# Splitting the second layer's weights: channel factors multiplied in place, 512 columns at once

## The chip, the cores and the metric

The kernel runs on one core of a Trainium2 chip. A core has a matrix engine (TensorE, PE in the profile; PEld is its loading of weights), a vector engine (VectorE, DVE), an activation engine (ScalarE, ACT), a general engine (GpSimd, POOL) and a queue engine that issues most of the transfers (SyncE, SP). Each engine works through its own list of instructions in order and waits on semaphores. The metric is the device time of one execution in microseconds, the median of several runs.

## The reference, cut to what matters

The reference is one step of a two-layer encoder over 1024 prompt tokens and 32 sample tokens (1056 in all), with 1024 channels. Layer 0 mixes tokens by pooling, layer 1 by differential attention; both attend to 256 memory tokens and end in a squared-ReLU MLP. Everything is float32.

```
h = rmsnorm(x, g_attn[l]);  z = h @ w_in[l]            # every layer
kv = rmsnorm(x, g_kv) @ w_kv                           # before layer 1: shared keys and values
rmsnorm(x, g) = x * rsqrt(mean(x*x) + 1e-6) * g        # g: one factor for each of the 1024 channels
```

In layer 1 the same x is normalised with two different sets of factors, `g_kv` for `w_kv` and `g_attn[1]` for `w_in[1]`. A factor on an input channel may as well be put on the row of the weight that this channel meets, and the factor of a token (the rsqrt) on the product. The kernel does so in layer 1: x is split once without factors, and each weight is multiplied by its column of factors.

## The kernel before, in words

TensorE multiplies float32 numbers in three passes. Each operand is split into a high part (`hi`, the number rounded to the type that TensorE reads, F32R) and a low part (`lo = number - hi`), and `mm3` (L48 to L54) issues hi·hi, hi·lo and lo·hi. The tokens lie in three groups of 352 columns (GW); a weight tile gives 128 output rows, from two halves of 128 x 512 numbers, which hold four blocks of 128 input channels each.

A weight goes through three stages. `weight_load` (L94) takes the next weight from the list in `weights` (L60) and starts the transfer of its two halves into buffers called `wraw`, of which there are six. `weight_split` (L121) calls `part` (L103) on each half: it writes `whi` and `wlo`, of which there are eight each. `weight` (L129) hands the split weight to the matmuls. A `wraw` buffer is free for the next transfer when the last instruction that reads it, the one that writes `wlo`, is done.

For most weights `part` is two instructions on 512 columns: a copy on ScalarE (L111) and a subtraction on VectorE (L112). For the 16 weights of layer 1 that carry factors (8 of `w_kv`, 8 of `w_in`, L78 to L84) it goes through the four blocks of a half one by one: ScalarE multiplies 128 columns by the factor and rounds (L116), VectorE multiplies again and subtracts (L117). The factor is one number for each partition and block, from the table `gains`.

The order of the instructions on each engine is set by a scheduler from the program's order, its data and its own estimates of durations; TensorE's order is fixed by it too. When an edit changes instructions, the scheduler may interleave all engines anew. The stages that matter here, in microseconds from the start of the profiled span:

- to about 930: the MLP of layer 0. Its last row of weights is split by L112, `b` at L1336 adds two partial sums of hidden activations.
- 930 to 975: the last part of the second MLP product (`ff2_last`): L1492 adds each finished tile to x, L57 and L58 split x into `xh` and `xl` for layer 1, L202 and L203 sum squares for the norm. The first `w_kv` halves are already loaded here. L1505 stores x to DRAM on the same SP queue that loads the weights.
- 975 to 1190: layer 1's projections and the differential attention. `diff_project` makes keys (`kst`, L722), values (`vst`, L734) and queries (`qf`, L743) from the PSUM tiles `dn`; these projections are the fill between score matmuls (L827, L828), transposes (L869) and products with values. VectorE makes the softmax's inputs (L834, L808) and the low parts `aTl` of the transposed probabilities (L58); ScalarE does the exponentials (L836) and the high parts `aTh` (L57). L212 makes the sums for the norms.

Of the kernel before, what the change touches and what calls it, by code (L numbers as in the profile page):

```python
# [10 lines left out]
F32 = mybir.dt.float32  # L11
F32R = mybir.dt.float32r
AF = mybir.ActivationFunctionType
ALU = mybir.AluOpType
# [29 lines left out]
class Kern:  # L44
# [58 lines left out]
    def part(self, src, eng, gcol=None):  # L103

        if self.wplace:
            hi, lo = self.wplace.pop(0), self.wplace.pop(0)
        else:
            hi = self.wpool.tile([128, 4, 128], F32R, tag="whi", name="whi", bufs=NW)
            lo = self.wpool.tile([128, 4, 128], F32R, tag="wlo", name="wlo", bufs=NW)
        if gcol is None:  # L110
            self.nc.scalar.copy(hi, src)  # L111
            eng.tensor_tensor(lo, src, hi.bitcast(F32), ALU.subtract)  # L112
            return hi, lo
        for c in range(4):
            gain = self.gains[:, gcol + c:gcol + c + 1]
            self.nc.scalar.mul(hi[:, c], src[:, c], gain)  # L116
            eng.scalar_tensor_tensor(lo[:, c], src[:, c], gain, hi[:, c].bitcast(F32), ALU.mult, ALU.subtract)  # L117
        return hi, lo

    def weight_split(self):  # L120
# [84 lines left out]
    def rstd(self, acc, n, r=None, pool=None, tile=None):  # L205

        nc = self.nc
        acc = acc if isinstance(acc, list) else [acc]
        N = acc[0].shape[-1]
        ps = (tile or self.stile)()[:, :N]  # L210
        for i, part in enumerate(acc):
            nc.tensor.matmul(ps, lhsT=self.ones, rhs=part, start=i == 0, stop=i == len(acc) - 1)  # L212
        y = (pool or self.base).tile([128, N], F32, tag="rs_y", name="rs_y", bufs=1)
        nc.scalar.activation(y, ps, AF.Ln, bias=self.epsc, scale=1.0 / n)
        nc.scalar.activation(y, y, AF.Exp, scale=-0.5)
        nc.vector.scalar_tensor_tensor(ps, ps, n * EPS, y, ALU.add, ALU.mult)
        nc.vector.scalar_tensor_tensor(ps, ps, -0.5 / n, y, ALU.mult, ALU.mult)
        nc.vector.scalar_tensor_tensor(ps if r is None else r, ps, 1.5, y, ALU.add, ALU.mult)
        return ps
# [1040 lines left out]
    def plan_weights(self, kind, b, at, loads, sums, parts):  # L1260


        nc = self.nc
        S = {}

        def raw(k):
            return self.raws[kind, b, k]

        def add(k):
            S[k] = S[2] if k == 4 else self.ph.tile([128, 4, 128], F32, tag="ws", name="ws", bufs=3)  # L1270
            x, y, op = ((2, 3, ALU.add), (1, 0, ALU.subtract), (0, 2, ALU.subtract), (1, 2, ALU.subtract))[k - 1]
            x = S[1] if k == 2 else raw(x)
            y = S[2] if k == 4 else raw(y)
            nc.vector.tensor_tensor(S[k], x, y, op)

        def part(k):
            src = S[int(k[1])] if k[0] == "S" else raw(("A11", "A12", "A21", "A22").index(k))
            self.A[kind, b, k] = self.part(src, self.low(kind, k))

        for k, o in enumerate(loads):  # L1280
            self.job(at + o, lambda k=k: self.block(kind, b, k))
        for k, o in enumerate(sums):
            self.job(at + o, lambda k=k: add(k + 1))
        for k, o in parts:
            self.job(at + o, lambda k=k: part(k))
# [424 lines left out]
```

## Time and profile before

| | us |
|---|---|
| median of 3 runs (2095.39 to 2095.83) | 2095.4 |
| the profiled execution, its own time | 2095.72 |
| span from its first to its last instruction | 2093.9 |
| TensorE busy | 2072.7 (99%) |
| VectorE busy | 1681.0 (80%) |
| ScalarE busy | 1125.8 (54%) |
| GpSimd busy | 567.3 (27%) |

The span is 1.8 us shorter than the execution's own time. Busy is the time in which an engine ran an instruction; one duration can overlap the next on the same engine, so the distance from start to start of neighbours is often shorter than the duration. Idle time of an engine costs nothing unless the engine that sets the end waits for it. Lines named L with a number are lines of the kernel before; the changed kernel has three lines fewer, so what stands below the change is there numbered three lower.

### The profile page before, as it was taken

Reading aid. Unit: us, or ns where it says so; the run is one execution under the profiler, and the core shown is the slowest. Engines: PE = TensorE matmul, PEld = TensorE weight load, DVE = VectorE, ACT = ScalarE, POOL = GpSimd, SP = SyncE. Lnnn points to the kernel's source line nnn. Section 1 sums busy time; section 2 is a strip of 40 time slices with the busy share of each in tenths; the row PEclk is TensorE's granted clock in tenths of the full one; section 3 lists DMA queues with packets and bytes.
Section 4 is the critical chain, followed back from the end, with each engine's and each line's share of the span. In section 5 each row is a group of like instructions: output and inputs, shape, how many; then the busy total and the mean of one; then the engine's idle time right before and its main releaser. Section 6 shows DMA issues by size and latency. Waiting matters only on the chain.

```text
span 2093.9 us, 35115 instructions
## 1 busy us (share of the span) xinstructions
PE 2072.7 (99%) x12961; PEld 2032.1 (97%) x12961; DVE 1681.0 (80%) x3156; ACT 1125.8 (54%) x2437; POOL 567.3 (27%) x577
## 2 busy tenths in 40 slices
PE   9999999999999999999999999999999999999997
PEld 8998999999999999999999998999999999999997
DVE  8856598888888888868778877588888888888865
ACT  7546364444444444456777766355444454444454
POOL 1021113343333333220111212104334333433323
PEclk9999999999999999999999999999999999999999
DMA  5635321111111111124222212411111111111112
GB/s 192 204 114 159 126 61 59 44 56 46 51 51 48 55 46 56 42 71 162 75 80 80 83 46 91 161 51 53 60 41 58 44 56 46 51 51 51 51 41 83
DMA packets 88140, 156.83 MB, mean 75 GB/s; under 512 B 12704, under 2 KB 29728, under 8 KB 87456
## 3 DMA queue, kind: packets, MB, share of 16 engines
q1 hardware_dynamic: 85952, 149.47, 22.3%
q10 hardware_dynamic: 2016, 5.13, 0.8%
q8 instruction: 101, 1.65, 0.3%
q14 instruction: 71, 0.58, 0.1%
HBM read 126.64 MB, written 23.72 MB: 72 GB/s over the span
## 4 chain that ended last, share of the span: by engine, by line
PE 89%; DVE 3%; ACT 3%; DMA 1%; issue 1%; POOL 0%; SPq 0%; DVEq 0%; ACTq 0%; POOLq 0%
PE dn L54 15%; PE dn L52 15%; PE dn L53 15%; PE mm L52 9%; PE mm L53 9%; PE mm L54 9%; PE xb L52 3%; PE xb L54 3%; PE xb L53 3%; PE sc L52 1%; PE sc L827 1%; PE sc L54 1%; PE sc L53 1%; PE mm L869 1%; PE sc L828 1%
## 5 line engine op out<-in xcount | busy, mean ns | idle before, releaser
L52 PE MATMUL dn<-xh,whi 128*128 128x352 f32 x1168 | 383.3, 328 | 3.0 <-ACT mvs L348 1.3
L54 PE MATMUL dn<-xh,wlo 128*128 128x352 f32 x1168 | 378.6, 324 | 0.0
L53 PE MATMUL dn<-xl,whi 128*128 128x352 f32 x1168 | 378.3, 324 | 0.2 <-DVE xl L233 0.2
L112 DVE TENSOR_TENSOR wlo<-wraw,whi 128x512 fp32r<-128x512 f32 x344 | 278.6, 813 | 86.9 <-ACT whi L111 86.1
L111 ACT CAST whi<-wraw 128x512 fp32r<-128x512 f32 x344 | 212.7, 620 | 233.4 <-PE dn L53 111.6
L1403 DVE TENSOR_TENSOR x<-x,mm 128x352 f32<-128x352 f32 x560 | 287.5, 513 | 63.1 <-PE mm L54 63.1
L52 PE MATMUL mm<-h2h,whi 128*128 128x352 f32 x832 | 270.4, 325 | 0.0
L54 PE MATMUL mm<-h2h,wlo 128*128 128x352 f32 x832 | 268.0, 322 | 0.0
L53 PE MATMUL mm<-h2l,whi 128*128 128x352 f32 x832 | 266.4, 320 | 0.0
L111 ACT CAST whi<-ws 128x512 fp32r<-128x512 f32 x232 | 143.8, 620 | 221.0 <-PE dn L53 123.4
L1403 DVE TENSOR_TENSOR x<-x,xb 128x352 f32<-128x352 f32 x448 | 222.9, 512 | 26.1 <-PE xb L54 23.4
L52 PEld LDWEIGHTS dn<-xh,whi 128*128 128x128 f32 x1168 | 219.5, 188 | 8.6 <-issue 2.1
L53 PEld LDWEIGHTS dn<-xl,whi 128*128 128x128 f32 x1168 | 220.7, 189 | 2.8 <-DVE xl L233 0.9
L54 PEld LDWEIGHTS dn<-xh,wlo 128*128 128x128 f32 x1168 | 220.1, 188 | 0.4
L58 POOL TENSOR_TENSOR h2l<-t,h2h 128x352 fp32r<-128x352 f32 x112 | 136.2, 1217 | 171.6 <-ACT h2h L57 171.6
L112 DVE TENSOR_TENSOR wlo<-ws,whi 128x512 fp32r<-128x512 f32 x232 | 179.2, 772 | 3.5 <-ACT whi L111 3.5
L58 POOL TENSOR_TENSOR h2l<-b,h2h 128x352 fp32r<-128x352 f32 x92 | 116.2, 1277 | 228.8 <-PE mm L54 204.1
L1387 POOL TENSOR_TENSOR t<-b,b 128x352 f32<-128x352 f32 x56 | 64.6, 1154 | 366.3 <-ACT b L1306 366.3
L53 PEld LDWEIGHTS mm<-h2l,whi 128*128 128x128 f32 x832 | 156.3, 188 | 0.4
L52 PEld LDWEIGHTS mm<-h2h,whi 128*128 128x128 f32 x832 | 156.1, 188 | 0.4
L54 PEld LDWEIGHTS mm<-h2h,wlo 128*128 128x128 f32 x832 | 156.2, 188 | 0.0
L54 PE MATMUL dn<-T,wlo 128*128 128x352 f32 x480 | 155.7, 324 | 0.0
(322 smaller groups left out, 5275.9 us busy)
## 6 DMA issues: line engine op xcount, KB each, us to landing
wraw<-in_w_ff SPq DMA_DIRECT2D x256, 256.0 KB, 2.6
wraw<-in_w_out SPq DMA_DIRECT2D x44, 256.0 KB, 3.6
wraw<-in_w_in SPq DMA_DIRECT2D x30, 256.0 KB, 3.5
o<-oscr SPq DMA_DIRECT2D x36, 176.0 KB, 3.2
xscr<-x SPq DMA_DIRECT2D x3, 1408.0 KB, 5.4
wraw<-in_w_mem SPq DMA_DIRECT2D x16, 256.0 KB, 3.0
wraw<-in_w_memv SPq DMA_DIRECT2D x16, 256.0 KB, 3.0
wraw<-in_w_kv SPq DMA_DIRECT2D x16, 256.0 KB, 2.9
```

Of the source, the lines that this page charges most:

```text
L52: mm(ps, lhsT=ah, rhs=bh, start=first, stop=False, skip_group_check=more)
L53: mm(ps, lhsT=ah, rhs=bl, start=False, stop=False, skip_group_check=more)
L54: self.last_mm = mm(ps, lhsT=al, rhs=bh, start=False, stop=last, skip_group_check=more)
L58: (lo_eng or self.nc.vector).tensor_tensor(lo, src, hi.bitcast(F32), ALU.subtract)
L111: self.nc.scalar.copy(hi, src)
L112: eng.tensor_tensor(lo, src, hi.bitcast(F32), ALU.subtract)
L827: nc.tensor.matmul(o, lhsT=q[:, c, 0, qc], rhs=KS[:, c, k:k + n], start=True, stop=False)
L828: nc.tensor.matmul(o, lhsT=q[:, c, 1, qc], rhs=KS[:, c, k:k + n], start=False, stop=True)
L869: nc.tensor.transpose(pt[:, 256 * a + 128 * i:256 * a + 128 * i + 128], A[i][:, k:k + 128], self.ident)
L1387: self.nc.gpsimd.tensor_tensor(h[out], h[a], h[c], ALU.subtract)
L1403: nc.vector.tensor_tensor(xj, xj, ps, ALU.add)
```

## The change

For a weight with factors, `part` now first multiplies the whole half (512 columns) by its factors on VectorE, in place in `wraw`; the factors are read with each one repeated over 128 columns. Then it copies to `whi` on ScalarE and subtracts into `wlo` on VectorE, as for every other weight.

```diff
         else:
             hi = self.wpool.tile([128, 4, 128], F32R, tag="whi", name="whi", bufs=NW)
             lo = self.wpool.tile([128, 4, 128], F32R, tag="wlo", name="wlo", bufs=NW)
-        if gcol is None:
-            self.nc.scalar.copy(hi, src)
-            eng.tensor_tensor(lo, src, hi.bitcast(F32), ALU.subtract)
-            return hi, lo
-        for c in range(4):
-            gain = self.gains[:, gcol + c:gcol + c + 1]
-            self.nc.scalar.mul(hi[:, c], src[:, c], gain)
-            eng.scalar_tensor_tensor(lo[:, c], src[:, c], gain, hi[:, c].bitcast(F32), ALU.mult, ALU.subtract)
+        if gcol is not None:
+            gain = self.gains[:, gcol:gcol + 4].unsqueeze(2).broadcast_to([128, 4, 128])
+            eng.tensor_tensor(src, src, gain, ALU.mult)
+        self.nc.scalar.copy(hi, src)
+        eng.tensor_tensor(lo, src, hi.bitcast(F32), ALU.subtract)
         return hi, lo
```

In the changed kernel the multiplication is line 112, the copy line 113 and the subtraction line 114. The scheduler interleaves anew. On VectorE, at the end of layer 0's MLP, where the last rows of its weights are split (`wlo<-wraw,whi`) and the last hidden sums `b` are added, there stands before:

```order
L1403 TENSOR_TENSOR x_2680<-x_2680,xb 128x352 x2
L112 TENSOR_TENSOR wlo<-wraw,whi 128x512 x2
L1336 TENSOR_TENSOR b_10646<-u_10624,dn 128x352
L112 TENSOR_TENSOR wlo<-wraw,whi 128x512
L1336 TENSOR_TENSOR b_10701<-u_10535,dn 128x352
L112 TENSOR_TENSOR wlo<-wraw,whi 128x512 x3
L1492 TENSOR_TENSOR x_2682<-x_2682,mm 128x352
```

and in the changed kernel, with the same names and lines three lower:

```order
L114 TENSOR_TENSOR wlo<-wraw,whi 128x512
L112 TENSOR_TENSOR wraw<-wraw,gains 128x512 x3
L1333 TENSOR_TENSOR b_10701<-u_10535,dn 128x352
L114 TENSOR_TENSOR wlo<-wraw,whi 128x512 x2
L112 TENSOR_TENSOR wraw<-wraw,gains 128x512
L114 TENSOR_TENSOR wlo<-wraw,whi 128x512
L112 TENSOR_TENSOR wraw<-wraw,gains 128x512
L1489 TENSOR_TENSOR x_2682<-x_2682,mm 128x352
L1489 TENSOR_TENSOR x_2682<-x_2682,dn 128x352
L58 TENSOR_TENSOR xl_10753<-x_2682,xh_10752 128x352
L112 TENSOR_TENSOR wraw<-wraw,gains 128x512
```

Six multiplications of layer 1's first three weights have moved up here; three of them stand ahead of the last sum `b`, two between the last splits and one after the first addition to x. All wait for the transfers of their halves. On VectorE again, where layer 1 begins and the first keys `kst` are taken from PSUM, there stands before:

```order
L203 TENSOR_TENSOR acc_10750<-acc_10750,sq 128x352
L58 TENSOR_TENSOR xl_11096<-x_2681,xh_11095 128x352
L117 SCALAR_TENSOR_TENSOR wlo<-wraw,gains,whi 128x128 x22
L275 TENSOR_SCALAR gsub<-gains 128x1
L722 TENSOR_TENSOR kst<-dn,rs_11003 128x352
L722 TENSOR_TENSOR kst<-dn,rs_11165 128x352
L779 TENSOR_TENSOR KS<-kst,KS 64x256
```

and in the changed kernel:

```order
L58 TENSOR_TENSOR xl_11086<-x_2681,xh_11085 128x352
L114 TENSOR_TENSOR wlo<-wraw,whi 128x512 x2
L112 TENSOR_TENSOR wraw<-wraw,gains 128x512 x3
L114 TENSOR_TENSOR wlo<-wraw,whi 128x512
L112 TENSOR_TENSOR wraw<-wraw,gains 128x512 x2
L272 TENSOR_SCALAR gsub<-gains 128x1
L719 TENSOR_TENSOR kst<-dn,rs_10993 128x352
L719 TENSOR_TENSOR kst<-dn,rs_11155 128x352
L112 TENSOR_TENSOR wraw<-wraw,gains 128x512 x2
```

Ahead of the first `kst` stand eight instructions of 512 columns in place of 22 of 128 columns, and two more multiplications stand behind the second `kst`. Further on, to about 1190 us, the multiplications stand one or two at a time between the softmax's instructions, and TensorE's order differs in where single projection matmuls stand between score and value matmuls; no matmul is added or removed.

## Rows read from the trace of the kernel before

**Rows 1.** The page, part 1: busy us of each engine, share, instructions.
```profile
PE 2072.7 (99%) x12961; PEld 2032.1 (97%) x12961; DVE 1681.0 (80%) x3156; ACT 1125.8 (54%) x2437; POOL 567.3 (27%) x577
```

**Rows 2.** Busy time by stretches: stretch, length, then each engine's busy us.
```profile
core 0: us, PE busy (x) PEld busy (x) DVE busy (x) ACT busy (x) POOL busy (x), PEclk, DMA share, GB/s
960.00:1190.00 230.00, 227.59 (x1461) 220.01 (x1460) 184.17 (x490) 167.93 (x439) 33.81 (x65) 1.00 0.33 101
```

**Rows 3.** Waits of PE, 960 to 1190: us in total, times, longest.
```profile
PE mm L53 <- DVE aTl L58: 0.7, 2, 0.4
PE mm L800 <- DVE std L841: 0.6, 1, 0.6
PE dn L52 <- DVE kst L722: 0.5, 1, 0.5
PE sc L827 <- DVE std L834: 0.2, 1, 0.2
PE mm L52 <- ACT aTh L57: 0.2, 1, 0.2
```

**Rows 4.** Lines L116 and L117: shortest, median, longest ns; first, last start.
```profile
L116 ACT ACTIVATE whi<-wraw,gains x128: 383/390/408, 964.6 to 1185.7; 128x128 fp32r<-128x128 f32 x128
L117 DVE SCALAR_TENSOR_TENSOR wlo<-wraw,gains,whi x128: 329/344/892, 965.1 to 1186.2; 128x128 fp32r<-128x128 f32 x128
```

**Rows 5.** Timeline of DVE and ACT: start, us, engine, line, how many merged.
```profile
976.17 3.34 ACT L116 ACTIVATE whi<-wraw,gains 128x128 fp32r<-128x128 f32 x11
...
976.81 5.86 DVE L117 SCALAR_TENSOR_TENSOR wlo<-wraw,gains,whi 128x128 fp32r<-128x128 f32 x22
...
1014.75 0.69 DVE L58 TENSOR_TENSOR V<-mm,V 128x512 fp32r<-128x512 f32 x1
1015.35 0.47 DVE L808 SCALAR_TENSOR_TENSOR pr<-pr,std 128x256 f32<-128x256 f32 x1
```

**Rows 6.** Lines L111, L112 and L912: shortest, median, longest ns.
```profile
L111 ACT CAST whi<-wraw x344: 602/620/661, 3.9 to 2033.3; 128x512 fp32r<-128x512 f32 x172
L112 DVE TENSOR_TENSOR wlo<-wraw,whi x344: 673/692/1439, 4.6 to 2034.0; 128x512 fp32r<-128x512 f32 x172
...
L912 DVE TENSOR_TENSOR sb<-sc,dists x1: 757/757/757, 1236.4 to 1236.4; 128x576 f32<-128x576 f32 x1
```

**Rows 7.** Waits of all engines, 960 to 1190: ScalarE's copies for a buffer.
```profile
ACT whi L116 <- PE dn L53: 7.8, 8, 4.0
```

**Rows 8.** Transfers issued from 915 to 930: KB each, median us to landing.
```profile
wraw<-in_w_kv SPq DMA_DIRECT2D x4, 256.0 KB, 2.9
```

**Rows 9.** Timeline of DVE, 916 to 931, end of layer 0's MLP.
```profile
919.08 0.69 DVE L112 TENSOR_TENSOR wlo<-wraw,whi 128x512 fp32r<-128x512 f32 x1
922.45 0.52 DVE L1336 TENSOR_TENSOR b<-u,dn 128x352 f32<-128x352 f32 x1 [2.69 <-PE dn L54]
...
929.78 0.52 DVE L1492 TENSOR_TENSOR x<-x,mm 128x352 f32<-128x352 f32 x1 [2.37 <-PE mm L54]
```

**Rows 10.** Timeline of ACT over the same stretch.
```profile
923.01 0.50 ACT L1305 ACTIVATE b<-b 128x352 f32<-128x352 f32 x1 [0.16 <-DVE b L1336]
...
926.06 0.62 ACT L111 CAST whi<-wraw 128x512 fp32r<-128x512 f32 x1 [0.98 <-PE dn L53]
```

**Rows 11.** Timeline of DVE and PE where layer 1's first keys are taken.
```profile
982.65 0.94 DVE L722 TENSOR_TENSOR kst<-dn,rs 128x352 f32<-128x352 f32 x2
...
983.22 0.43 PE L52 MATMUL dn<-xh,whi 128*128 128x352 f32 x1 [0.49 <-DVE kst L722]
```

**Rows 12.** Line L1274: ns; idle before it until a transfer (us, times).
```profile
L1274 DVE TENSOR_TENSOR ws<-wraw x116: 675/940/1436, 294.0 to 1995.4; 128x512 f32<-128x512 f32 x116
...
  DMA wraw<-in_w_ff: 22.6, 28
```

## The prediction

> **What bounds the kernel now.** I read the page's busy times first. TensorE is busy for 2072.7 of 2093.9 us, VectorE for 80% and ScalarE for 54% [rows 1]. So the end is set by TensorE's list of matmuls, and an edit that adds or removes no matmul can shorten the run only by time in which TensorE waits. Next I looked where the touched lines run: both start between 964.6 and 1186.2 us [rows 4]. In the stretch 960 to 1190 TensorE is busy for 227.59 of 230 us, VectorE for 184.17, ScalarE for 167.93, and the granted clock is 1.00 [rows 2]. TensorE is idle for 2.4 us there, and the table of its waits accounts for 2.2 of them: 0.7, 0.6, 0.5 and 0.2 us on VectorE's results, 0.2 us on ScalarE's [rows 3]. None of these waits is for `whi` or `wlo`. The split weights are always ready in time; what the change lightens, TensorE does not wait for.
>
> **The work taken away and put in.** 16 weights of two halves are 32 halves. Before, each takes four instructions on each of two engines: 128 on ScalarE and 128 on VectorE [rows 4]. After, ScalarE has 32 copies, and VectorE 32 multiplications and 32 subtractions.
>
> ScalarE: eleven L116 in a row take 3.34 us, 0.304 us from one to the next [rows 5], so 128 are 38.9 us. A copy of 512 columns takes 0.62 us [rows 6], 32 are 19.8 us. ScalarE saves some 19 us. TensorE can get from that at most the 0.2 us that it waited for ScalarE [rows 3]; ScalarE's work otherwise lies beside matmuls.
>
> VectorE: 22 L117 in a row take 5.86 us, 0.266 us each [rows 5]; 128 are 34.1 us. A subtraction on 512 columns lasts 0.692 us [rows 6], but the next instruction behind one of that size starts 0.60 us after it (1014.75 to 1015.35) [rows 5], so 64 take 38.4 us: 4.3 us more. Six of the multiplications now stand around 930 us, outside the stretch; in the stretch it is 58 x 0.60 = 34.8 us against 34.1, which is 0.7 us more on an engine that has 45.8 us idle there [rows 2]. The multiplication itself isn't in the trace of before. Its lower bound is the 0.692 us of a subtraction of the same size; as upper bound I take the longest of those, 1.439 us [rows 6]. The nearest row to a repeated operand is L912, which reads one operand twice over (once for each half of its columns): 576 columns in 0.757 us, against 0.692 us for 512 without repetition [rows 6], so 65 ns for 64 more columns and nothing for the repetition. I take 0.692 us (0.60 from start to start). At the upper bound 26 multiplications in the stretch cost VectorE 26 x 0.75 = 19.5 us more.
>
> Finer grain lost: what stands behind one of the new instructions waits up to 0.60 - 0.27 = 0.33 us longer than behind an L117. If that hit each of the five waits of TensorE [rows 3] it would cost 1.7 us; if the new order removes them all, it gains 2.2. I take +0.4 us.
>
> From the moment a `whi` buffer is free, a half took four L116 and the last L117, 4 x 0.304 + 0.344 = 1.6 us; now it takes a copy and a subtraction, 0.62 + 0.69 = 1.3 us, since the multiplication needs no `whi` and can be done earlier. ScalarE waited eight times, 7.8 us in all, for such a buffer [rows 7]. So weights come some 0.3 us sooner there, and `wraw` buffers come free as much sooner. As TensorE waits for neither, this is worth 0.
>
> **The multiplications that moved up.** This is where the change adds waits. The third one ahead of `b` needs a half whose buffer comes free when the subtraction that starts at 919.08 ends, at 919.77 [rows 9]. The transfer lands 2.9 us later [rows 8], at 922.7, and the multiplication ends about 0.6 us after that, 923.3. Behind it in VectorE's list stands `b`, which started at 922.45 [rows 9]: it comes 0.85 us late. ScalarE's L1305 waited for it at 923.01 and then had 0.98 us idle before 926.06, where it waits for TensorE [rows 10]. The delay is smaller than that idle time, so ScalarE meets TensorE at 926.06 as before, and what TensorE needs next comes as before. With the cover gone it would cost up to 0.85 us; I take 0. The multiplications between the last splits delay the last `wlo` by about a microsecond; its matmuls belong to the second half of the output tiles, and VectorE's next duty is at 929.78, for which it waited 2.37 us [rows 9]. I take 0.
>
> **The first keys of layer 1.** Before, 22 L117 stand ahead of `kst` at 982.65, and TensorE waits 0.49 us for it [rows 11]. Now there are eight instructions, 8 x 0.60 = 4.8 us in place of 5.86, so `kst` could come 1.1 us earlier and the 0.49 us would go. But the last two of the five multiplications wait for halves whose buffers come free only shortly before, and a transfer takes 2.9 us [rows 8]; that may put them a microsecond late. Between -0.5 and +1.0 I take 0.
>
> A rule that speaks against the change: the two-input instructions share something with GpSimd. The trace has L112 at 0.692 us in the median and 1.439 at the longest, L117 at 0.344 and 0.892 [rows 4, 6], and GpSimd is busy for 33.81 of the 230 us [rows 2]. The Trainium skill (SBUF — State Buffer, "Who interferes with whom") says that a VectorE instruction with two SBUF inputs and a GpSimd instruction that reads SBUF exclude each other for the whole instruction, so that longer ones block longer; by it, the estimate is 58 x 0.15 x 0.75 = 6.5 us lost on VectorE here. The same estimate for the 128 L117 is 128 x 0.15 x 0.55 = 10.6 us, so the rule's own difference favours the change, and TensorE would see little of either.
>
> **The sum.** Against the profiled execution's own 2095.72 us: ScalarE's relief -0.1 (0 to -0.2), VectorE's grain and load +0.4 (-2.2 to +2.4, which is 1.7 + 0.7), the moved multiplications 0 (0 to +0.85), the first keys 0 (-0.5 to +1.0). That is 2096.0. The profiled execution lies 0.3 us above the median of 2095.4, so in runs I expect 2095.7 to 2096; I say 2096.0. The bounds added up give 2092.8 to 2100.0 with all on one side; the likeliest case's own range is 2094 to 2099.
>
> **The rivals.**
> Same, as worked out: 80%. I call "same" what lies within 0.2%, 4.2 us, of 2095.4 (2091.2 to 2099.6); a measurement of this kernel can hardly tell less.
>
> Slower, multiplications that wait at the head of VectorE's list: a multiplication is now the first reader of a fresh half, so a late transfer stops VectorE, and with it PSUM tiles that TensorE needs emptied; before, ScalarE stood in front. What speaks for it: L1274, which reads fresh halves on VectorE too, waited 28 times in 116 for the transfer, 22.6 us in all, 0.81 us each time [rows 12]. Against: the scheduler has put the multiplications where the half should be there, and VectorE has idle time. The place is the attention stage after 1010 us, where by the order 14 multiplications stand among the softmax's instructions. If all of them waited 0.81 us and TensorE paid in full, it is 11.3 us, 2107; at half of them 5.7 us, 2101.5, which I take for this case. It decides from the point where one wait is longer than TensorE's lead over the PSUM tile behind it. 13%.
>
> Slower, the repeated factors are read slowly: 1.439 us in place of 0.692. That takes 19.5 of VectorE's 45.8 idle us; TensorE pays perhaps a quarter, as an estimate, and the time is 2101, at most 2115. Against it stands L912. 4%.
>
> Faster beyond 0.2%: all of TensorE's idle time in the stretch is 2.4 us, which gives 2093.3 and is still "same". More would need stages whose order barely changed to run better. 3%.
>
> **The numbers.** Faster 0.03, same 0.80, slower 0.13 + 0.04 = 0.17. The range has to hold the first case and reach into the slower ones: 2093.5 to 2103. Below it lies perhaps 0.05, above it about 0.09.
>
> **What the profile of the changed kernel would show.** Right: 32 copies of about 0.62 us and 64 two-operand instructions of about 0.69 us on VectorE; in 960 to 1190 ScalarE's busy time down by some 20 us, VectorE's within a few us of 184, TensorE's idle time still 1 to 5 us. `b` starts near 923.3 with a multiplication waiting for a transfer in front of it, and no new wait of TensorE near 930. Wrong: multiplications at 1 us or more without GpSimd at work; waits of VectorE for `in_w_kv` or `in_w_in` of more than 8 us in all with TensorE's waits for `kst`, `qf`, `aTl` or `std` growing with them; or TensorE's idle time in the stretch above 6 us.

## The result, and the profile after

The changed kernel takes 2101.42 us in the median of seven runs (2099.13 to 2102.36), the kernel before beside it 2095.39 us (2094.29 to 2095.83): 6.0 us more, a ratio of 1.0024 with a 95% interval of 1.0015 to 1.0033. That lies inside the predicted range and above the likeliest case, which was said to end at 2099.6 us: the kernel became slower, by about the amount that was given for the 13% rival. The profiled execution of the changed kernel took 2102.36 us, its span 2100.4.

The page's busy times and the stretch of the attention, in the form of [rows 1] and [rows 2] (stretch, its length, busy us of PE, PEld, DVE, ACT and POOL, granted clock, DMA share, GB/s):

```profile
PE 2076.5 (99%) x12961; PEld 2035.0 (97%) x12961; DVE 1687.6 (80%) x3092; ACT 1106.3 (53%) x2341; POOL 573.1 (27%) x577
```

```profile
960.00:1190.00 230.00, 225.18 (x1433) 216.81 (x1432) 183.34 (x410) 144.75 (x332) 37.77 (x64) 1.00 0.31 98
```

ScalarE's load falls as expected, by 19.5 us in the whole run. VectorE's load in the stretch is what it was. TensorE's idle time there is 230 - 225.18 = 4.8 us; before it was 2.4. The table of its waits, in the order of [rows 3], says for what:

```profile
PE dn L52 <- DVE kst L719: 1.8, 1, 1.8
PE mm L797 <- DVE V L58: 0.9, 1, 0.9
PE mm L53 <- DVE aTl L58: 0.8, 1, 0.8
PE mm L52 <- ACT aTh L57: 0.6, 1, 0.6
PE sc L824 <- DVE std L831: 0.4, 1, 0.4
```

The wait for the first keys has grown from 0.5 to 1.8 us, and a new one for the values `V` is there, where the kernel before waited 0.6 us for `std`. The multiplication itself costs what its lower bound said. The view of its line (shortest, median and longest ns; then the idle time ahead of it, us and times):

```profile
L112 DVE TENSOR_TENSOR wraw<-wraw,gains x32: 679/691/1222, 921.2 to 1134.6; 128x512 f32<-128x512 f32 x32
...
  DMA wraw<-in_w_in: 5.1, 8
  DMA wraw<-in_w_kv: 3.5, 5
```

The median is 0.691 us, so the repeated factors cost nothing. But 13 of the 32 stood waiting for their transfer, 8.6 us in all, and what stood behind them in VectorE's list waited as well. Three places show what came of it. The first is the end of layer 0's MLP, VectorE's timeline (start, length, idle time before it and what ended it); it answers to [rows 9]:

```profile
922.63 1.05 DVE L112 TENSOR_TENSOR wraw<-wraw,gains 128x512 f32<-128x512 f32 x1 [0.78 <-DMA wraw<-in_w_kv]
923.87 1.22 DVE L112 TENSOR_TENSOR wraw<-wraw,gains 128x512 f32<-128x512 f32 x1 [0.19 <-DMA wraw<-in_w_kv]
925.01 0.51 DVE L1333 TENSOR_TENSOR b<-u,dn 128x352 f32<-128x352 f32 x1
...
928.78 0.69 DVE L112 TENSOR_TENSOR wraw<-wraw,gains 128x512 f32<-128x512 f32 x1 [0.96 <-DMA wraw<-in_w_kv]
929.39 0.69 DVE L114 TENSOR_TENSOR wlo<-wraw,whi 128x512 fp32r<-128x512 f32 x1
```

GpSimd beside them, ScalarE's copy that answers to the one at 926.06 in [rows 10], and the matmul that needs GpSimd's last result:

```profile
922.18 0.94 POOL L58 TENSOR_TENSOR h<-b,h 128x352 fp32r<-128x352 f32 x1 [4.41 <-ACT h L57]
923.59 0.95 POOL L58 TENSOR_TENSOR h<-b,h 128x352 fp32r<-128x352 f32 x1 [0.46 <-PE dn L53]
...
929.52 1.34 POOL L58 TENSOR_TENSOR h<-g,h 128x352 fp32r<-128x352 f32 x1 [0.89 <-ACT h L57]
```

```profile
927.41 0.62 ACT L113 CAST whi<-wraw 128x512 fp32r<-128x512 f32 x1
```

```profile
930.92 0.43 PE L53 MATMUL mm<-h,whi 128*128 128x352 f32 x1 [0.67 <-POOL h L58]
```

In the kernel before, the same instruction of GpSimd and the same matmul:

```profile
928.17 0.94 POOL L58 TENSOR_TENSOR h<-g,h 128x352 fp32r<-128x352 f32 x1 [2.58 <-ACT h L57]
```

```profile
929.16 0.43 PE L53 MATMUL mm<-h,whi 128*128 128x352 f32 x1 [0.27 <-POOL h L58]
```

Two multiplications are stretched from 0.69 to 1.05 and 1.22 us, each to 0.55 us behind the end of the GpSimd instruction that overlaps it (923.12 and 924.54). This is as the Trainium skill has it (SBUF — State Buffer, "Who interferes with whom"): a VectorE instruction with two inputs from SBUF and a GpSimd instruction that reads SBUF shut each other out.

To compare the times, 1.35 us have to be taken off, by which this execution was already behind (see below). `b` then starts 1.2 us late, and that costs TensorE nothing: ScalarE's copy at 927.41 is the 926.06 of before, and GpSimd starts `h` from `g` at 929.52, the 928.17 of before. What costs is the last multiplication shown, at 928.78. It waits 0.96 us for its transfer, and the subtraction behind it, at 929.39, falls beside GpSimd's `h`, at a time when VectorE was idle before [rows 9]: `h` takes 1.34 us instead of 0.94, and the matmul comes 0.41 us late. In the other kernels below, `h` takes 1.33 to 1.37 us where this multiplication stands, and 0.93 or 0.94 where it doesn't.

The second place is the first keys, to be laid beside [rows 11] and the row of 22 L117 in [rows 5]:

```profile
979.26 1.28 DVE L114 TENSOR_TENSOR wlo<-wraw,whi 128x512 fp32r<-128x512 f32 x2
980.46 1.89 DVE L112 TENSOR_TENSOR wraw<-wraw,gains 128x512 f32<-128x512 f32 x3
982.27 0.68 DVE L114 TENSOR_TENSOR wlo<-wraw,whi 128x512 fp32r<-128x512 f32 x1
983.68 0.69 DVE L112 TENSOR_TENSOR wraw<-wraw,gains 128x512 f32<-128x512 f32 x1 [0.73 <-DMA wraw<-in_w_in]
985.04 0.69 DVE L112 TENSOR_TENSOR wraw<-wraw,gains 128x512 f32<-128x512 f32 x1 [0.67 <-DMA wraw<-in_w_in]
...
985.72 0.94 DVE L719 TENSOR_TENSOR kst<-dn,rs 128x352 f32<-128x352 f32 x2
```

```profile
986.28 0.43 PE L52 MATMUL dn<-xh,whi 128*128 128x352 f32 x1 [1.80 <-DVE kst L719]
```

The two multiplications ahead of `kst` wait 0.73 + 0.67 = 1.40 us for transfers; neither weight is needed by TensorE yet. The third place is the first values, where a multiplication stands ahead of `V` in the same way:

```profile
1016.10 1.01 DVE L112 TENSOR_TENSOR wraw<-wraw,gains 128x512 f32<-128x512 f32 x1 [0.92 <-DMA wraw<-in_w_kv]
...
1017.38 1.28 DVE L58 TENSOR_TENSOR V<-mm,V 128x512 fp32r<-128x512 f32 x2
```

```profile
1018.20 0.27 PE L797 MATMUL mm<-ident,vst 128*32 128x128 f32 x1 [0.89 <-DVE V L58]
```

To see where the time goes I laid the traces side by side: the start of the same matmul (counted from the first) in a kernel, less its start in the kernel before. Each row of this table begins at 0 at 908.7 us, ahead of the change's first effect; it tells how many us later the matmul comes than it should. The columns are times in the kernel before.

```
                                          931.2  984.9  1013.0  1071.1  1205.8  1442.4
changed kernel                            +0.41  +1.73   +2.09   +3.51   +5.05   +5.11
first 14 halves new, 18 old               +0.43  +1.89   +3.63   +3.72   +3.78   +3.28
first 14 old, last 18 new                 +0.01  +0.03   +0.38   +2.19   +3.81   +3.99
new, without the multiplication            0.00  -0.75   -0.39   -0.49   +0.35   +0.78
new, copy ahead of the multiplication      0.00  +1.44   +1.45   +2.83   +3.24*  +0.91
new, multiplications behind the keys      +0.43  -0.32   +0.05   -0.12   +1.17*  +0.49
  the same for the first head alone       +0.43  -0.32   +0.05   +2.25   +3.74   +4.04
  the same behind the values too  +0.39  -0.36   +0.01   -0.15   +1.87*  +1.27
  the same, first four halves old         +0.01  -0.74   -0.38   -0.39   +0.89*  +0.71
old, products behind the keys              0.00  -0.75   -0.38   -0.46   +2.64*  +2.69
  the same for the first head alone       +0.01  -0.74   -0.38   -0.40   -0.35   -0.21
ScalarE multiplies                        +0.02  -0.76   -0.39   -0.20   +1.27   +1.82
GpSimd multiplies                         +0.10  -0.65   +4.25   +4.17   +5.12   +5.13
* TensorE's order differs at this count: another matmul, so a rough value
```

The loss of the changed kernel has a beginning and an end: 0.4 us at `h`, 1.3 at the first keys, 0.4 in small steps from there to 1013, 0.4 at the first values (their matmul in the last row above comes 3.88 us after its start in the kernel before, 2.5 by the count of the table), and the other half, 2.5 us, in small steps inside the attention up to 1206, nothing behind. The three places are 2.1 of 5.1 us; for the small steps no single reason is shown. A further 1.35 us of the difference between the two profiled executions had come before 908.7, mostly between 219 and 298 us, where the order of the instructions is the same in both. I count it to the executions and not to the kernels: in the other profiled kernels the same matmul comes between 2.15 us earlier and 1.18 us later than in the kernel before.

### The profile page after: what moved, and what is told of

It reads as the page before. It is cut to its first block, busy times and chain, and to the rows that moved or that the text cites. A ratio compares the mean times of both kernels' runs of the same rounds, so it can differ in the third digit from the quotient of the medians.

```text
span 2100.4 us, 34950 instructions
## 1 busy us (share of the span) xinstructions
PE 2076.5 (99%) x12961; PEld 2035.0 (97%) x12961; DVE 1687.6 (80%) x3092; ACT 1106.3 (53%) x2341; POOL 573.1 (27%) x577
## 3 DMA queue, kind: packets, MB, share of 16 engines
q8 instruction: 101, 1.65, 0.3%
## 4 chain that ended last, share of the span: by engine, by line
PE 89%; DVE 3%; ACT 3%; DMA 1%; issue 1%; POOL 0%; SPq 0%; DVEq 0%; ACTq 0%; POOLq 0%
PE dn L54 15%; PE dn L52 15%; PE dn L53 15%; PE mm L52 9%; PE mm L53 9%; PE mm L54 9%; PE xb L52 3%; PE xb L54 3%; PE xb L53 3%; PE sc L824 1%; ACT pr L576 1%; PE sc L52 1%; PE sc L825 1%; PE mm L866 1%; PE sc L54 1%
## 5 line engine op out<-in xcount | busy, mean ns | idle before, releaser
L114 DVE TENSOR_TENSOR wlo<-wraw,whi 128x512 fp32r<-128x512 f32 x376 | 300.7, 804 | 91.4 <-ACT whi L113 90.6
L113 ACT CAST whi<-wraw 128x512 fp32r<-128x512 f32 x376 | 232.1, 620 | 250.1 <-PE dn L53 124.6
```

## The experiments

Three theories. **1:** what a multiplication holds up is what stands behind it in VectorE's list; where that is a result for which TensorE waits soon, TensorE pays. In its narrow form the reason is the wait for the transfer. **2:** VectorE's load has grown, wherever it stands. **3:** every new interleaving costs or gains a few us, whatever moved. All times are medians, each kernel against the kernel before run on the same chip, 7 to 11 runs of each edited one.

**Half of the change at a time.** The first kernel has the new path for the first 14 halves, the second, with `<= 14`, for the last 18. For the other halves the old branch stays:

```diff
+        self.nfac = getattr(self, "nfac", 0) + (gcol is not None)
+        if gcol is not None and self.nfac > 14:
+            for c in range(4):
+                gain = self.gains[:, gcol + c:gcol + c + 1]
+                self.nc.scalar.mul(hi[:, c], src[:, c], gain)
+                eng.scalar_tensor_tensor(lo[:, c], src[:, c], gain, hi[:, c].bitcast(F32), ALU.mult, ALU.subtract)
+            return hi, lo
```

> The new path for the first 14 factored halves (those of the seven weights up to the first keys), the old path of four blocks for the other 18. Theory 1 (a multiplication is the first reader of a fresh half and stops VectorE's list until the half's transfer is there) and theory 2 (VectorE's slots are longer) put the drift of the two traces up to 986 us here: 0.4 us at the state update near 929 and 1.3 us at the first keys, so about +1.7 us over the kernel before, ratio 1.0008 (1.0003 to 1.0012), and PE waits about 1.8 us for kst as in the changed kernel. Theory 3 (any new interleaving of the lists costs a few us, whatever moved) gives no such split: ratio anywhere between 1.000 and 1.003.

> The old path for the first 14 factored halves, the new path for the last 18, which are split inside the attention. Theories 1 and 2: the rest of the drift, 5.0 - 1.7 = about +3.3 us, ratio 1.0016 (1.0010 to 1.0021); PE waits at the first keys as in the kernel before (0.5 us), and at V about 0.9 us with a multiplication ahead of it that waits for its transfer. The two halves of the experiment should add up to the whole (1.0024). Theory 3: no such sum.

Measured: 2097.61 us for the first 14 (+2.1, ratio 1.0009, interval 1.0000 to 1.0018) and 2098.84 for the last 18 (+3.4, 1.0018, 1.0009 to 1.0027). Together 5.5 of the 6.0 us, which fits a loss that is a sum over places. It is no proof: each interval is about 1.9 us wide to either side, and 1.4 us of the first kernel's profile is a price that the changed kernel didn't pay (last section). In the first kernel TensorE waits 1.77 us for `kst` as in the changed one; in the second the first keys are as before and the table's steps inside the attention are back. The wait expected for `V` isn't in the table as such: at the same matmul TensorE waits 1.0 us for `std`, which stands behind `V` and behind a multiplication that waited 0.48 us for its transfer. Theory 3 gave no reason for such a sum, but isn't excluded by it.

**Without the multiplication.**

```diff
-            eng.tensor_tensor(src, src, gain, ALU.mult)
+            pass
```

> The new path without its multiplication (this leaves the channel factors of the second layer's weights out of the computation); the copy and the subtraction over 512 columns stay. ScalarE's copy is then the first reader of a half, VectorE has 32 instructions of about 0.69 us in place of 128 of 0.27 us. Theories 1 and 2 agree: the loss goes, ratio 0.9985 to 1.0002 (2092.3 to 2095.8 us), PE idle between 960 and 1190 at most 2.5 us. A theory that the coarse copy and subtraction alone delay what stands behind them: still 1.001 to 1.002. Theory 3: 1.000 to 1.003.

Measured: 2096.39 us (+0.9, ratio 1.0004, 0.9995 to 1.0013), a little above what theories 1 and 2 expected. Most of the loss is gone, but VectorE's shorter list brings no gain either: the table shows 0.75 us won at the first keys, where TensorE now waits for nothing, and some 1.3 us given back between 1071 and 1442. So the coarser copy and subtraction may have a price of their own inside the attention; the new order that came with them may as well be the reason, and the runs themselves can't be told from no change.

**The copy first, then the multiplication, then the subtraction.**

```diff
+        self.nc.scalar.copy(hi, src)
         if gcol is not None:
             gain = self.gains[:, gcol:gcol + 4].unsqueeze(2).broadcast_to([128, 4, 128])
             eng.tensor_tensor(src, src, gain, ALU.mult)
-        self.nc.scalar.copy(hi, src)
```

> The same three instructions for each half, but ScalarE's copy first, then the multiplication, then the subtraction (the high part is then that of the unscaled weight, so the split is not the reference's). VectorE does the same work in the same number of instructions as in the changed kernel, but is no longer the first reader of a half: the copy is. Theory 1: VectorE's waits for in_w_kv and in_w_in (8.6 us in the changed kernel) fall under 2 us and most of the loss goes, ratio 1.000 to 1.001, unless a wait for the copy takes their place. Theory 2: the same load, the same loss, 1.002 to 1.003.

Measured: 2099.86 us (+4.4, ratio 1.0019, 1.0010 to 1.0028). This is a miss of theory 1 in its narrow form: the multiplication waits for no transfer any more, and most of the loss stays. VectorE's group of multiplications (count, busy us, mean ns, then idle time before them), its timeline ahead of the first keys, and TensorE's matmul there:

```profile
L113 DVE TENSOR_TENSOR wraw<-wraw,gains 128x512 f32<-128x512 f32 x32 | 22.4, 710 | 5.1 <-ACT whi L110 5.0
```

```profile
977.01 1.29 DVE L113 TENSOR_TENSOR wraw<-wraw,gains 128x512 f32<-128x512 f32 x2
978.22 1.29 DVE L114 TENSOR_TENSOR wlo<-wraw,whi 128x512 fp32r<-128x512 f32 x2
979.42 1.29 DVE L113 TENSOR_TENSOR wraw<-wraw,gains 128x512 f32<-128x512 f32 x2
980.62 1.29 DVE L114 TENSOR_TENSOR wlo<-wraw,whi 128x512 fp32r<-128x512 f32 x2
981.83 0.68 DVE L113 TENSOR_TENSOR wraw<-wraw,gains 128x512 f32<-128x512 f32 x1
982.55 0.69 DVE L114 TENSOR_TENSOR wlo<-wraw,whi 128x512 fp32r<-128x512 f32 x1
...
983.22 0.94 DVE L719 TENSOR_TENSOR kst<-dn,rs 128x352 f32<-128x352 f32 x2
```

```profile
983.79 0.43 PE L52 MATMUL dn<-xh,whi 128*128 128x352 f32 x1 [1.93 <-DVE kst L719]
```

The wait for the copy takes the place of the wait for the transfer (5.0 us), and ahead of `kst` VectorE works without a pause on five multiplications and five subtractions. So a transfer at the head of the list is not needed for the loss. The single profile taken, the fastest of the eleven executions at 2096.25 us, shows 3.2 us lost to 1206 and most of it won back by 1442, with another order of matmuls there; what the slower executions do is not known.

**The same instructions in another order.** In the program four multiplications precede the first keys; the scheduler had drawn eight more ahead. This kernel forbids it, with every instruction as in the changed kernel; the scheduler then interleaves the rest anew, TensorE's order too:

```diff
-            nc.vector.tensor_tensor(kst[:, g * GW:(g + 1) * GW], ps, self.rs[g], ALU.mult)
+            self.behind = nc.vector.tensor_tensor(kst[:, g * GW:(g + 1) * GW], ps, self.rs[g], ALU.mult)
...
-            eng.tensor_tensor(src, src, gain, ALU.mult)
+            with self.tc.issue_after(self.behind.ins) if getattr(self, "behind", None) else ExitStack():
+                eng.tensor_tensor(src, src, gain, ALU.mult)
```

> The changed kernel, with one constraint on VectorE's order: the multiplications that the program writes after a head's keys stand behind the last instruction that writes those keys (four stand ahead of the first keys, in place of twelve). The load of every engine stays. Theory 1 (what the multiplications hold up is what stands behind them in VectorE's list): PE's wait for kst (1.8 us) falls under 0.5, the first part of the loss (1.3 to 1.7 us) goes, the part inside the attention stays: 2097.5 to 2099.8 us, ratio 1.0010 to 1.0021. Theory 2 (VectorE's load is the cost, wherever it stands): the wait comes back at the next values or keys, 1.0020 to 1.0030. If the held multiplications make the values' weights late, PE shows a wait for wlo or whi that neither kernel has.

Measured: 2095.74 us, +0.15, ratio 1.0000 (0.9991 to 1.0008): the whole loss is gone, more than was expected. In the stretch of the attention (columns as above), with TensorE's waits and VectorE's multiplications there:

```profile
960.00:1190.00 230.00, 228.92 (x1458) 220.34 (x1457) 183.00 (x420) 147.06 (x340) 37.97 (x65) 1.00 0.32 100
```

```profile
PE mm L798 <- DVE std L839: 0.5, 1, 0.5
PE mm L53 <- DVE aTl L58: 0.2, 1, 0.2
```

```profile
L113 DVE TENSOR_TENSOR wraw<-wraw,gains 128x512 f32<-128x512 f32 x28 | 18.7, 699 | 0.1
```

VectorE's load is that of the changed kernel (183.00 against 183.34 us), TensorE's idle time 1.1 against 4.8 us, and the 28 multiplications there wait 0.1 us for anything. Theory 2 falls: the load is not the cost. The order is; which part of it is not separated, since the rest of the order moved along.

At the first keys nothing stands ahead now, and VectorE waits for TensorE instead of the reverse; the multiplications follow in the next gap:

```profile
977.98 0.52 DVE L720 TENSOR_TENSOR kst<-dn,rs 128x352 f32<-128x352 f32 x1 [1.35 <-PE dn L54]
981.85 0.52 DVE L720 TENSOR_TENSOR kst<-dn,rs 128x352 f32<-128x352 f32 x1 [3.34 <-PE dn L54]
...
987.28 1.89 DVE L113 TENSOR_TENSOR wraw<-wraw,gains 128x512 f32<-128x512 f32 x3
```

The same with the values as well as the keys (`self.behind` is also set by the instruction that writes `vst`):

> As the one before, but the multiplications stand behind the last instruction that writes the keys or the values, whichever the program wrote last before them. Theory 1: as there or better, 2096.0 to 2099.5 us (1.0003 to 1.0019), since the multiplications now stand up to 15 us later, when their transfers have long landed: VectorE's waits for in_w_kv and in_w_in fall from 8.6 us under 4. Theory 2: 1.0020 to 1.0030 whatever the waits do. Against both: weights too late for PE, over 1.003 with PE waits for wlo.

Measured: 2096.22 us (+0.6, ratio 1.0004, 0.9995 to 1.0013); VectorE's multiplications wait 2.1 us in all, as against 8.6 in the changed kernel and 1.9 with the keys alone. No better than that one.

**The constraint for the first head alone** (`self.behind` is cleared when the next head's keys are written):

> The constraint on VectorE's order for the first head alone: the eight multiplications that stood ahead of the first keys early stand behind them, the other heads' are ordered freely as in the changed kernel. If the loss is made of many places (theory 1 as the drift of the traces gave it: 1.7 us up to the first keys, 3.3 us inside the attention), about 3 us stay: 2098.0 to 2099.5 us, 1.0011 to 1.0020, with PE waits for V, aTl or std as in the changed kernel. If nearly all hangs on the first keys and on the order that follows from them, it is as with the constraint for all heads: 2095.3 to 2096.7 us, 0.9998 to 1.0006.

Measured: 2100.60 us (+5.6, ratio 1.0028, 1.0017 to 1.0039). Beyond both expectations: the first keys are repaired as with all heads, and the loss comes back from one place further on. VectorE and TensorE at the first values:

```profile
1012.90 1.08 DVE L113 TENSOR_TENSOR wraw<-wraw,gains 128x512 f32<-128x512 f32 x1 [1.65 <-DMA wraw<-in_w_kv]
...
1014.25 1.28 DVE L58 TENSOR_TENSOR V<-mm,V 128x512 fp32r<-128x512 f32 x2
```

```profile
1015.08 0.27 PE L799 MATMUL mm<-ident,vst 128*32 128x128 f32 x1 [1.92 <-DVE V L58]
```

Here the transfer at the head of the list is the reason, by the row: 1.65 us idle ahead of a multiplication, then `V`, 1.92 us of TensorE. With the constraint for all heads no multiplication stands there, and the wait is not there.

**The multiplication on another engine.** On ScalarE in four blocks, and on GpSimd whole:

```diff
-            eng.tensor_tensor(src, src, gain, ALU.mult)
+            for c in range(4):
+                self.nc.scalar.mul(src[:, c], src[:, c], self.gains[:, gcol + c:gcol + c + 1])
```

```diff
-            eng.tensor_tensor(src, src, gain, ALU.mult)
+            self.nc.gpsimd.tensor_tensor(src, src, gain, ALU.mult)
```

> ScalarE multiplies the four blocks in place (128 instructions; the old ones of this form took 0.33 us, 42.2 / 128), then copies 512 columns (0.62 us) and VectorE subtracts once: VectorE has 32 instructions in place of 64 (after) or 128 (before), ScalarE about 20 us more than before (32 x 0.62). Theories 1 and 2: VectorE's list is that of the kernel without multiplication, so no PE wait for kst, 2095.0 to 2097.5 us (0.9998 to 1.0010), unless ScalarE's list, 168 + 17 of 230 us busy in the attention, now holds up aTh, KS or the exponentials: PE waits for ACT would then grow over 1 us and the time be over 2098.

> The multiplication on GpSimd instead of VectorE (its rows of two operands with 352 columns take 1.0 to 1.28 us in the kernel before, so about 1.5 to 2.0 us for 512: 48 to 64 us in all, of 34 busy in the 230 us of the attention). The waits for the transfers move to GpSimd's list. Theory 1: no PE wait for kst or V behind them, 2095.5 to 2098 us (1.0000 to 1.0012). Theory 2: the same for VectorE's load, less what the two engines cost each other: VectorE's subtractions beside a multiplication longer than 0.69 us. Against: GpSimd is slow enough to make Q or the weights late: over 1.002 with PE waits that begin at POOL.

ScalarE: 2096.35 us (+0.8, ratio 1.0005, 0.9996 to 1.0014), as expected; one execution of the eleven took 5354.76 us, which nothing here explains, the others 2095.64 to 2098.54. ScalarE's multiplications wait 7.8 us for transfers, and in TensorE's table of waits from 900 to 1210 us no result of ScalarE appears; the other table shows the same 0.75 us won at the keys and then some 2 us given back as without the multiplication. GpSimd: 2099.54 us (+4.0, ratio 1.0020, 1.0011 to 1.0029), a miss of theory 1, which expected at most 2098. VectorE is relieved, and yet TensorE waits 2.73 us for `kst`, of the third group this time:

```profile
987.75 1.07 DVE L264 TENSOR_TENSOR lq<-lq 128x128 f32<-128x128 f32 x1 [4.83 <-DMA lq<-in_lam]
...
989.18 0.99 DVE L776 TENSOR_TENSOR KS<-kst,KS 64x256 fp32r<-64x256 f32 x1
...
992.84 0.52 DVE L719 TENSOR_TENSOR kst<-dn,rs 128x352 f32<-128x352 f32 x1
```

The small `lq` takes 1.07 us instead of 0.29 and `KS` 0.99 instead of 0.42 beside GpSimd's multiplications (1.04 us each from 985.5 to 989.9), and two subtractions stand ahead of the third `kst`. The long wait for the transfer of `lq` is not new: in the kernel before it ends at 987.65.

**Is the constraint worth something by itself?** The kernel before, with the old L117 held behind the keys, for all heads and for the first alone; and the changed kernel with the constraint and the first four halves old:

```diff
-            eng.scalar_tensor_tensor(lo[:, c], src[:, c], gain, hi[:, c].bitcast(F32), ALU.mult, ALU.subtract)
+            with self.tc.issue_after(self.behind.ins) if getattr(self, "behind", None) else ExitStack():
+                eng.scalar_tensor_tensor(lo[:, c], src[:, c], gain, hi[:, c].bitcast(F32), ALU.mult, ALU.subtract)
```

> The kernel before, with the same constraint: its small instructions of VectorE that the program writes after a head's keys stand behind them (6 in place of 22 right ahead of the first keys). The kernel before shows a PE gap of 0.95 us there, of which 0.5 us is a wait for kst; without it 2094.3 to 2095.2 us, 0.9994 to 0.9998. If it gains that much, the changed kernel with the constraint, which is even with the kernel before, still carries about 0.5 to 1 us from the new path. If it gains nothing or loses (a later start of the weights of the values), the new path with the constraint costs nothing.

> The kernel before, its old path of four blocks untouched, with the constraint for the first head alone (6 of VectorE's small instructions right ahead of the first keys in place of 22, the other heads ordered freely). If the order ahead of the first keys is worth what PE's gap there shows (0.95 us before, 0.1 where the constraint stood) and nothing pays for it later, 2094.2 to 2094.9 us, 0.9994 to 0.9998: faster than both kernels. If the held instructions only move the loss to the next place, as with the new path (first values: gap 2.24 us), or the later heads' order changes with it, 2095.5 to 2098 us, and the gaps at 1122 and 1180 us of the kernel with the constraint for all heads (1.2 and 1.4 us) show which of the two.

> The changed kernel with the constraint for all heads, and the first four factored halves by the old path of four blocks, since with the new one PE's gap ahead of h grew from 0.59 to 1.01 us near 929 (GpSimd's instruction there took 1.34 us beside VectorE's, 0.94 before). That gap back at 0.59: 0.4 us less than with the constraint alone, 2095.0 to 2095.7 us, 0.9996 to 1.0001; below the kernel before by what the PE wait for kst was there (0.5 us). A change of 0.4 us is at the edge of what the intervals hold, so the gap itself decides.

The old path with the constraint for all heads: 2097.73 us (+2.7, ratio 1.0011, 1.0001 to 1.0020), slower, against the expectation. The gap at the first keys is gone; new ones stand at 1122.6 us (1.21 us from one matmul's start to the next, a wait for ScalarE's `aTh`) and at 1181:

```profile
1181.91 0.36 PE L828 MATMUL sc<-KS,Q 128*128 128x256 f32 x1 [1.12 <-DMA Q<-Q]
```

So theory 3 has a share: with no multiplication in the program at all, an order rule of the same kind costs 2.7 us elsewhere. For the first head alone: 2094.51 us against 2095.19 (-0.7, ratio 0.9998, 0.9989 to 1.0007). The gap is gone, of the 0.74 us won there 0.4 are left at 1071 and 0.2 at 1442, and the time can't be told from no change; no kernel tried is shown to beat the one before. The third: 2096.74 us (+1.7, 1.0007, 0.9998 to 1.0015). Its gap at `h` is back at 0.59 us as expected, and the multiplications in the stretch wait 0.1 us for anything; the time is above what was expected and no better than with the constraint alone, so 0.4 us at one place doesn't show.

## Why the prediction was right, and where not

The range held, by the room that was left in it for the slower rivals; the likeliest case, at 80%, didn't.

- **What bounds the kernel:** right. TensorE's list sets the end; ScalarE's 19 us (measured 19.5) bought nothing.
- **The multiplication's cost:** right at the lower bound, 0.691 us; the rival with slowly read factors is out. VectorE's load in the stretch changed by -0.8 us where +0.7 was reckoned, and the constrained kernel shows that this load costs TensorE nothing.
- **"The moved multiplications 0":** wrong by 0.4 us, and not where the risk was seen. The transfer came as reckoned; the second and third multiplication took 1.05 and 1.22 us beside GpSimd, so that `b` started 1.2 us late instead of 0.85. That still cost nothing: less the 1.35 us, ScalarE made its copy at 926.06 as reckoned. What failed is the second zero, for the multiplications between the last splits: the prediction asked when VectorE has its next duty, and not what GpSimd does meanwhile. GpSimd's `h`, for which TensorE waits, took 1.34 us instead of 0.94 beside the delayed subtraction. The rule on the two engines was in the prediction, but priced for VectorE's time alone.
- **"The first keys 0":** the step that failed most clearly, 1.3 us, beyond its upper bound of +1.0. The eight instructions were counted, and the risk of the last two transfers named; the middle of two bounds was taken although the order already showed two multiplications of fresh halves directly ahead of a result for which TensorE was waiting even before [rows 11].
- **"Grain and load +0.4":** mis-sized. From 985 to 1442 us the changed kernel lost 3.4 us. The kernels without the multiplication, or with it on ScalarE, put 1.3 and 2.0 us of loss behind 1071 although VectorE does less there; in the changed kernel 0.4 us more come with the multiplication ahead of `V`. How much belongs to the coarser instructions and how much to the multiplications is not settled, since each kernel has its own interleaving.
- **The 13% rival:** its direction and sign came true (8.6 us of waits, above the 8 that were named as a sign, with TensorE's waits for `kst`, `V`, `aTl` and `std` growing). Its 2101.5 us met the measured time by luck, not by its reckoning: 13 waits, not 7 of 14, many at places where nothing urgent stood behind, and three places where TensorE's rows show that it paid, 2.1 us in all, one of them by way of GpSimd. And the copy-first kernel shows that the wait for the transfer is one way in which a multiplication holds up the list, not the only one. What is shown is the wider cause: with the same instructions in an order that keeps multiplications away from the keys, the loss is gone. That an order rule of this kind moved the kernel before by 2.7 us, with no multiplication in it, says how much of such a difference the interleaving alone can make.

## What to carry to other kernels

An edit that lightens an engine which nobody waits for has next to nothing to gain and may lose. Ask of each new instruction not only what it takes but which engine's list it joins and what stands behind it: on an engine that makes results for the bottleneck, work that isn't needed yet, above all the first reader of a transfer, belongs behind those results, and one ordering rule may be worth more than the edit. Such a rule isn't free either: try it for the whole stage, since at one place it can move the wait to the next. Ask also what runs beside the new instruction on the engine that it shuts out, and who waits for that.

## What the runs showed of the hardware

The same gap of TensorE at the first keys had two prices. In the kernel with the first 14 halves new, TensorE was idle for 1.77 us ahead of the matmul at 984.10, and then the granted clock fell (columns as above):

```profile
982.00:984.00 2.00, 0.33 (x2) 0.00 (x0) 1.33 (x5) 0.55 (x1) 0.00 (x0) 1.00 1.02 409
984.00:986.00 2.00, 1.91 (x11) 1.91 (x12) 1.38 (x4) 0.81 (x2) 0.21 (x1) 0.90 0.49 173
986.00:988.00 2.00, 2.00 (x8) 2.00 (x8) 1.90 (x7) 1.03 (x3) 0.00 (x0) 0.50 0.00 0
988.00:990.00 2.00, 2.00 (x11) 2.00 (x11) 1.51 (x4) 1.24 (x4) 0.00 (x0) 0.75 0.00 0
990.00:992.00 2.00, 2.00 (x14) 2.00 (x13) 1.66 (x4) 0.78 (x3) 0.00 (x0) 1.00 0.70 212
```

0.50 is the lower of the two levels, 1.2 GHz. The matmuls lose another 1.4 us: in the table this kernel goes from +1.89 at 985 to +3.63 at 1013, 1.7 us, and the changed kernel in the same stretch by 0.4. The profiled execution of the changed kernel had a gap of 1.80 us at the same place and kept 1.00 behind it, and so did the copy-first kernel with 1.93 us and the first-head kernel with its 1.92 us at the first values; the GpSimd kernel with 2.73 us fell to 0.50 too. So a wait of two microseconds may cost nearly the double, in some executions and not in others. The eleven runs of the first kernel spread from 2095.5 to 2101.4 us; whether this is why isn't shown, and the kernel before spread from 2094.0 to 2098.6 beside them.
